# A log-softmax that streams 3.3 GB through one DMA queue: one store in four sent as two halves around the next load

## The chip, the core and the metric

The kernel runs on one core of one Trainium2 chip. The core has a matrix engine (PE), a vector engine (DVE), a scalar engine (ACT), a general-purpose engine (POOL) and a sync engine (SP), which here issues all transfers. Transfers are carried by 16 DMA engines. The metric is device time in microseconds; the time of a kernel is the median of its runs.

## The reference

For an array `x` of 16 × 512 rows of 50000 float32 numbers:

```python
def reference(x):
    max_x = np.max(x, axis=-1, keepdims=True)
    shifted = x - max_x
    log_sum_exp = np.log(np.sum(np.exp(shifted), axis=-1, keepdims=True))
    return (shifted - log_sum_exp).astype(np.float32)
```

The input is 1638.4 MB and so is the output. Every number is read once and written once.

## The kernel before

**Tiles.** The 8192 rows are cut into 256 tiles of 32 rows. A row is spread over four of the 128 partitions, so a tile is 128 partitions × 12500 numbers (50,000 bytes in a partition, 6250 KB in all). Four buffers (`bufs[0]` to `bufs[3]`) hold four tiles; tile t lives in buffer t mod 4, and the result overwrites the input in place.

**Compute.** For each tile DVE waits until it has landed, takes the negated maximum of four pieces of 3125 columns (`negm`, L206), combines them over the four partitions of each row (L211, L174 to L189), and later subtracts maximum and log-sum in one instruction over the whole tile (L194). ACT takes the exponentials with their sums (L242), the scale factors (L250) and the logarithm (L236). PE adds the sums over the partitions of a row (L270). DVE goes from one tile to the next strictly in order.

**Transfers.** SP runs a program written out by hand (L151 to L167). It loads the first four tiles and stores tile 0. Then a loop of 63 rounds follows with four steps each. Step j, with k the next buffer after j, does this, in this order: wait until buffer k's result is ready (`subtracted[k]`), issue its store; wait until the store of buffer j, issued one step earlier, has completed (`stored[j]`, which counts 16 for one transfer); issue the load of a new tile into buffer j. All waits go through one helper, `take` (L45), which waits for a count and subtracts it. SP does one thing after the other: while it waits, nothing behind the wait is issued. Transfers of SP go into one queue. I write S1 for the store of buffer 1 and L0 for the load of buffer 0; a round is then S1 L0 S2 L1 S3 L2 S0 L3. After the loop the last tiles are stored, the very last one in four pieces of 3125 columns.

Of the kernel before, what the change touches and what calls it, by code (L numbers as in the profile page):

```python
# [42 lines left out]
def take(engine, sem, n=16):  # L43

    engine.wait_ge(sem, n).then_inc(sem, -n)  # L45


def cols(c):
    return slice(c * C, (c + 1) * C)
# [3 lines left out]
def kernel(  # L53
# [9 lines left out]
    W = V // G  # L63
# [10 lines left out]
    def run(a, first, n):  # L74

        part = a[first : first + NBUF * n].rearrange("(q i) p w -> q i p w", i=NBUF)
        return lambda q, i: part[bass.ds(q, 1), i].rearrange("o p w -> (o p) w")
# [13 lines left out]
    bufs = [data.tile([P, W], FP32, name=f"buf{j}") for j in range(NBUF)]  # L91
# [19 lines left out]
    def sem(name):  # L111
        return ctx.enter_context(nc.semaphore(name))

    landed = [sem(f"landed{j}") for j in range(NBUF)]
    stored = [sem(f"stored{j}") for j in range(NBUF)]
# [13 lines left out]
    @block.gpsimd  # L129
    def _(gpsimd):  # L130
        view = ones.rearrange("p (r g) -> p r g", g=G)
        gpsimd.memset(ones, 1.0).then_inc(ready)  # L132
        gpsimd.affine_select(  # L133
            out=view, in_=view, pattern=[[-G, R], [0, G]], base=0,
            channel_multiplier=1, compare_op=ALU.is_ge, fill=0.0,
        ).wait_op(ready, 1, "sem-ge").then_inc(ready)
        gpsimd.affine_select(  # L137
            out=view, in_=view, pattern=[[G, R], [0, G]], base=G - 1,
            channel_multiplier=-1, compare_op=ALU.is_ge, fill=0.0,
        ).wait_op(ready, 2, "sem-ge").then_inc(ready)  # L140

    @block.sync
    def _(sync):
        def load(j, src):
            sync.dma_start(out=bufs[j], in_=src).then_inc(landed[j], 16)

        def store(j, dst, buf):
            take(sync, subtracted[j], 1)
            sync.dma_start(out=dst, in_=buf).then_inc(stored[j], 16)

        for t in range(NBUF):  # L151
            load(t, xt[t])
        store(0, ot[0], bufs[0])
        src, dst = run(xt, NBUF, rounds), run(ot, 1, rounds)
        with sync.Fori(0, rounds) as q:
            for j in range(NBUF):
                k = (j + 1) % NBUF
                store(k, dst(q, j), bufs[k])
                take(sync, stored[j])
                load(j, src(q, j))  # L160
        for j in range(1, NBUF - 1):
            store(j, ot[ntiles - NBUF + j], bufs[j])
        for c in range(NS):
            store(NBUF - 1, ot[ntiles - 1][:, cols(c)], bufs[NBUF - 1][:, cols(c)])
        for j in range(NBUF - 1):
            take(sync, stored[j])
        take(sync, stored[NBUF - 1], 16 * NS)  # L167
# [147 lines left out]
```

## Time and profile before

| what | value |
|---|---|
| median of 5 runs | 7593.84 us (7593.16 to 7594.87) |
| profiled execution | 7593.36 us |
| its span, first to last instruction | 7591.7 us |
| DVE busy | 5440.2 us, 72% |
| ACT busy | 3184.7 us, 42% |
| PE busy | 477.9 us, 6% |
| HBM read and written | 1638.40 MB each, 432 GB/s over the span |
| SP's waits in `take` (L45) | 7301.9 us in 512 waits |

The page gives busy time by engine, then the span in 40 slices with the busy share of the DMA engines in tenths and the rate, then the DMA queues (packets, MB, share of the time of 16 engines), groups of instructions by line, and the transfers by kind with their size and the median time from issue to landing. The timeline lists instructions in order of time: start, duration, engine, line, operation, and in brackets the idle time before it and who ended it. A packet is one contiguous piece moved by one DMA engine: 50,000 bytes, one partition's share of a tile. A transfer of 128 partitions gives each of the 16 engines eight of them, followed by one small packet that adds 1 to the transfer's semaphore.

### The profile page before, as it was taken

What the parts mean: (1) busy time and instruction counts of PE and PEld (TensorE: products, weight loads), DVE (VectorE), ACT (ScalarE), POOL (GpSimd) and SP (SyncE); (2) the same over time, 40 slices, a digit from 0 to 9 for tenths busy, and PEclk for the clock granted to TensorE, in tenths of its full rate; (3) what the DMA queues carried; (4) which work ended last, traced back from release to release, by engine and by line L of the source; (5) the groups of instructions that cost most, each with busy time, mean ns of one, the idle gap of its engine ahead of it and who ended that gap; (6) DMA issues with size and microseconds to landing.
All of it is one profiled execution on the core that took longest, in us unless ns stands there. A gap on an engine that the chain in (4) does not pass through costs nothing. (4 is left out here: it accounts for less than half of the span.)

```text
span 7591.7 us, 14139 instructions
## 1 busy us (share of the span) xinstructions
PE 477.9 (6%) x2048; PEld 455.9 (6%) x2048; DVE 5440.2 (72%) x2819; ACT 3184.7 (42%) x2561; POOL 1.4 (0%) x7
## 2 busy tenths in 40 slices
PE   0000000000000000000000000000000000000000
PEld 0000000000000000000000000000000000000000
DVE  7777777777777777777777777777777777777776
ACT  4444443434444344443444434444344443434433
POOL 0000000000000000000000000000000000000000
DMA  9999999999999999999999999999999999999999
GB/s 425 432 432 433 432 434 433 432 433 433 432 433 433 433 433 433 433 432 434 432 434 432 434 433 433 433 433 433 433 432 433 433 433 433 433 433 433 433 433 392
DMA packets 74162, 3276.85 MB, mean 432 GB/s; under 512 B 8240, under 2 KB 8240, under 8 KB 8240
## 3 DMA queue, kind: packets, MB, share of 16 engines
q1 hardware_dynamic: 74160, 3276.83, 100.0%
q14 instruction: 2, 0.02, 0.0%
HBM read 1638.40 MB, written 1638.40 MB: 432 GB/s over the span
## 5 line engine op out<-in xcount | busy, mean ns | idle before, releaser
L242 ACT ACTIVATE dump<-buf,negm 128x3125 f32<-128x3125 f32 x1024 | 2937.2, 2868 | 3804.2 <-DVE negm L206 3706.7
L206 DVE TENSOR_REDUCE negm<-buf 128x1 f32<-128x3125 f32 x1024 | 3418.3, 3400 | 922.7 <-DVEq L45 922.7
L194 DVE TENSOR_SCALAR buf<-buf,negmax,logsum 128x12500 f32<-128x12500 f32 (+1 forms) x259 | 1738.8, 6715 | 554.0 <-ACT logsum L236 554.0
L270 PE MATMUL sums<-scaled,ones 128*128 128x1 f32 x2048 | 477.9, 355 | 7086.6 <-DVE scaled L217 7086.6
L270 PEld LDWEIGHTS sums<-scaled,ones 128*128 128x128 f32 x2048 | 455.9, 328 | 7108.4 <-DVE scaled L217 7108.4
L217 DVE TENSOR_TENSOR scaled<-scale,part 128x4 f32<-128x4 f32 x256 | 41.4, 162 | 580.4 <-ACT scale L250 580.4
L236 ACT ACTIVATE logsum<-sums 128x1 f32<-128x1 f32 x256 | 43.8, 171 | 551.1 <-PE sums L270 551.1
L242 ACT ACTIVATION_READ_ACCUMULATOR dump<-buf,negm 128x1 f32 x1024 | 190.9, 186 | 0.0
L250 ACT ACTIVATE scale<-negm,negmax 128x4 f32<-128x4 f32 x256 | 76.1, 297 | 23.6
L211 DVE TENSOR_REDUCE negp<-negm 128x1 f32<-128x4 f32 x256 | 40.1, 157 | 39.2 <-DVE negm L206 39.2
L189 DVE STREAM_TRANSPOSE negmax<-spread 128x32 f32<-128x32 f32 x256 | 54.2, 212 | 8.9
L174 DVE STREAM_TRANSPOSE allneg<-negp 128x32 f32<-128x32 f32 x256 | 54.1, 211 | 8.9
L177 DVE TENSOR_REDUCE rowneg<-allneg 128x8 f32<-128x32 f32 x256 | 47.5, 186 | 8.9
L183 DVE COPY spread<-rowneg 128x32 f32<-128x32 f32 x256 | 46.3, 181 | 8.9
L257 ACT ACT_TABLE_LOAD x1 | 1.3, 1283 | 1.0 <-SPq L109 1.0
L137 POOL TENSOR_SCALAR_AFFINE_SELECT ones<-ones 128x128 f32<-128x128 f32 x1 | 0.5, 518 | 0.1
L133 POOL TENSOR_SCALAR_AFFINE_SELECT ones<-ones 128x128 f32<-128x128 f32 x1 | 0.5, 517 | 0.1
L132 POOL MEMSET ones<- 128x128 f32 x1 | 0.2, 204 | 0.5 <-SPq L109 0.5
L299 POOL MEMSET const-bfloat16-1.0<- 128x1 bf16 x1 | 0.1, 101 | 0.0
L299 POOL MEMSET const-uint8-127<- 128x1 uint8 x1 | 0.1, 101 | 0.0
L299 POOL MEMSET const-float32-0.0<- 128x1 f32 x1 | 0.1, 98 | 0.3 <-issue 0.3
L299 POOL MEMSET const-float32-1.0<- 128x1 f32 x1 | 0.1, 98 | 0.0
## 6 DMA issues: line engine op xcount, KB each, us to landing
buf<-in_x_dram SPq DMA_DIRECT2D x256, 6250.0 KB, 44.2
out_dram<-buf SPq DMA_DIRECT2D x255, 6250.0 KB, 47.8
out_dram<-buf SPq DMA_DIRECT2D x4, 1562.5 KB, 11.7
```

What stands on the lines that cost most here:

```text
L174: vector.transpose(out=allneg, in_=negp.to_broadcast([P, SQ]))
L177: vector.tensor_reduce(out=rowneg, in_=allneg.rearrange("p (r g) -> p r g", g=G), op=ALU.min, axis=AX,)
L183: vector.tensor_copy(out=spread.rearrange("p (r g) -> p r g", g=G), in_=rowneg[:, :, None].to_broadcast([P, SQ // G, G]),)
L189: vector.transpose(out=negmaxs[k], in_=spread)
L194: ins = vector.tensor_scalar(out=buf, in0=buf, scalar1=negmaxs[k][:, 0:1], scalar2=logs[k], op0=ALU.add, op1=ALU.subtract,)
L206: vector.tensor_reduce(out=negms[j][:, c : c + 1], in_=bufs[j][:, cols(c)], op=ALU.max, axis=AX, negate=True,).then_inc(shifted.sem if c < ...
L211: vector.tensor_reduce(out=negp, in_=negms[j], op=ALU.min, axis=AX).then_inc(on_dve.sem)
L217: vector.tensor_mul(out=scaleds[j], in0=scales[j], in1=parts[j])
L236: scalar.activation(out=logs[k], in_=rowsums[k], func=ACT.Ln)
L242: scalar.activation(out=dump, in_=bufs[j][:, cols(c)], func=ACT.Exp, bias=negms[j][:, c : c + 1], scale=1.0, accum_out=parts[j][:, c : c + 1],
L250: scalar.activation(out=scales[j], in_=negms[j], func=ACT.Exp, bias=negmaxs[j][:, 0:1], scale=-1.0,)
L270: ins = tensor.matmul(rowsums[j], ones, scaleds[j][:, c : c + 1], start=c == 0, stop=c == NS - 1,)
```

## The change

In step j=0 of each round, the store of buffer 1 is issued as two transfers, columns 0 to 6249 and columns 6250 to 12499. The first is issued where the whole store was. The second is issued after the load of buffer 0. Both add to `stored[1]`, so the wait of step j=1, ahead of the load into buffer 1, is for 32 instead of 16. The order in a round becomes S1a L0 S1b S2 L1 S3 L2 S0 L3. Nothing else differs: not the compute engines' programs, and not what SP does before and after the loop.

```diff
         src, dst = run(xt, NBUF, rounds), run(ot, 1, rounds)
+        half = [slice(0, W // 2), slice(W // 2, W)]
         with sync.Fori(0, rounds) as q:
             for j in range(NBUF):
                 k = (j + 1) % NBUF
-                store(k, dst(q, j), bufs[k])
-                take(sync, stored[j])
+                if j == 0:
+                    store(k, dst(q, j)[:, half[0]], bufs[k][:, half[0]])
+                else:
+                    store(k, dst(q, j), bufs[k])
+                take(sync, stored[j], 32 if j == 1 else 16)
                 load(j, src(q, j))
+                if j == 0:
+                    sync.dma_start(
+                        out=dst(q, j)[:, half[1]], in_=bufs[k][:, half[1]]
+                    ).then_inc(stored[k], 16)
```

## The prediction

> **What bounds the kernel now.** I read the page from its second part, because no engine of the first part is near full (DVE 72%).
>
> ```profile
> span 7591.7 us, 14139 instructions
> ...
> DMA  9999999999999999999999999999999999999999
> GB/s 425 432 432 433 432 434 433 432 433 433 432 433 433 433 433 433 433 432 434 432 434 432 434 433 433 433 433 433 433 432 433 433 433 433 433 433 433 433 433 392
> ...
> q1 hardware_dynamic: 74160, 3276.83, 100.0%
> ...
> buf<-in_x_dram SPq DMA_DIRECT2D x256, 6250.0 KB, 44.2
> out_dram<-buf SPq DMA_DIRECT2D x255, 6250.0 KB, 47.8
> out_dram<-buf SPq DMA_DIRECT2D x4, 1562.5 KB, 11.7
> ```
>
> The 16 DMA engines are busy in every slice, at one rate, and all of it is the one queue q1. A transfer is 6250 KB and lands 44 to 48 us after its issue, while 432 GB/s moves it in 14.8 us: three transfers stand in line. The order of issue, one round of the loop (the SP part of the timeline of 3008 to 3128 us; columns are start, duration, instruction):
>
> ```profile
> 3008.49 0.34 SPq L149 DMA_DIRECT2D out_dram<-buf  x1
> 3026.84 0.35 SPq L145 DMA_DIRECT2D buf<-in_x_dram  x1
> 3038.09 0.34 SPq L149 DMA_DIRECT2D out_dram<-buf  x1
> 3056.49 0.35 SPq L145 DMA_DIRECT2D buf<-in_x_dram  x1
> 3067.73 0.34 SPq L149 DMA_DIRECT2D out_dram<-buf  x1
> 3086.11 0.35 SPq L145 DMA_DIRECT2D buf<-in_x_dram  x1
> 3097.29 0.34 SPq L149 DMA_DIRECT2D out_dram<-buf  x1
> 3115.76 0.35 SPq L145 DMA_DIRECT2D buf<-in_x_dram  x1
> 3127.03 0.34 SPq L149 DMA_DIRECT2D out_dram<-buf  x1
> ```
>
> 101 stores were issued before the first row, so it is store number 101, counted from 0: buffer 1, step j=0. The rows are S1 L0 S2 L1 S3 L2 S0 L3, then S1 again 118.54 us later. That is eight transfers of 14.82 us; the DMA sets the period. The vector engine has slack in it, which its own rows show for one tile:
>
> ```profile
> 3001.45 6.79 DVE L194 TENSOR_SCALAR buf<-buf,negmax,logsum 128x12500 f32<-128x12500 f32 x1 [2.17 <-ACT logsum L236]
> ...
> 3011.89 13.35 DVE L206 TENSOR_REDUCE negm<-buf 128x1 f32<-128x3125 f32 x4 [3.65 <-DVEq L45]
> ```
>
> After each subtraction DVE waits 3.65 us for the next tile to land (the wait on `landed`, taken at L45).
>
> **One DMA engine is behind the other fifteen.** A transfer ends with sixteen small semaphore packets, one for each engine. In the trace's landing events fifteen engines lead the last one by 2 to 4 us in the first rounds, by 11 us at most in round 40, by 18 us in round 62: 0.30 us a round. Its packets follow each other every 1850.7 ns on average, those of the others every 1846.5 (single packet records around 7150 us). So the end belongs to this engine, and the tail shows it alone. The DMA view of 7583 to 7589 us:
>
> ```profile
> DMA packets 14, 0.16 MB, mean 27 GB/s; under 512 B 1, under 2 KB 1, under 8 KB 1
> ## 3 DMA queue, kind: packets, MB, share of 16 engines
> q1 hardware_dynamic: 14, 0.16, 6.4%
> ```
>
> 6.4% of 16 engines is one engine. Its whole run adds up to the span: first packet at 2.0 us, 511 whole transfers of 14.82 us (7573), four quarter stores 15.14, then 1.9 us to the span's end: 7592 against 7591.7. Whatever lengthens this engine's packets is paid in full; whatever only moves instructions is paid nothing as long as its ring has work.
>
> **The change, part by part.**
>
> 1. *63 more DMAs, in 63 rounds.* Store 1 becomes two, of 25,000 B a row in place of 50,000. Each DMA engine gets 16 half rows instead of 8 whole ones, and one semaphore packet more. No half row is in the trace; the nearest row is the last tile, stored in four quarters of 12,500 B. On the lagging engine its four semaphore packets follow that of the store before it by 3.788, 3.783, 3.800 and 3.773 us: 15.144 us for a tile. Whole stores on the same engine take 14.86 us in steady state (semaphore packet at 7200.30 to 7215.15). The difference, 0.28 us, pays for 24 more row pieces and 3 more semaphore packets; a half split adds 8 and 1, a third: 0.095 us. On the other engines a quarter row takes 471.2 ns to the next packet, a whole one 1846.5: (4 × 471.2 − 1846.5)/3 = 12.8 ns a piece, × 8, + 6 ns for the semaphore packet (9 ns long, 3 overlapped) = 0.108 us. I take 0.10 us a round: 63 × 0.10 = **6.3 us**. Lower bound: the shortest quarters (464 ns) against the shortest wholes (1843 ns) give 4.3 ns a piece, 0.041 us a round, 2.6 us. Upper bound: quarter rows were stored with no loads beside them for the most part, half rows will be stored beside loads on other engines; I allow double, 0.2 us, 12.6 us. The quarters begin at offsets 12,500, 25,000 and 37,500 B in a row, so the halves' offset is among them, and is no dearer there.
>
> A rule that speaks against the change: the Trainium skill, "DMA: Bandwidth & Descriptors", Anatomy of one DMA, gives about 2.0 us fixed for every DMA, most of it the wait until the last write is confirmed. Paid here, that is 63 × 2.0 = 126 us, and 7720 us. The trace disagrees: on the busy ring the packet after a semaphore packet starts 6 ns after that packet's start, and packets overlap by 3 ns. With transfers in line the receipt of one lies under the next. I take the row, and keep the rule for a ring that runs empty.
>
> 2. *Load 0 goes ahead of half a store.* In the queue: before S1 L0 S2 L1, after S1a L0 S1b S2 L1. The bytes before S2 are the same, so S2 and all behind it keep their places. L0 lands 7.4 us earlier (36.8 us after issue instead of 44.2). DVE can use 3.65 us of that, since it is busy until then; S0's subtraction ends about 3093.6 instead of 3097.2, S0 is still behind L2 (issued 3086.1) in line, and then DVE waits some 7.3 us for tile 1, which lands no earlier. Gain: nothing. Changes of direction between load and store stay eight a round. SP's one more issue (0.34 us) falls in its waits: SP waited 7301.9 us of the span.
>
> 3. *The wait for 32 moves the issue of load 1.* S1b lands where L0 landed, about 3071.0, so L1 is issued at 3071.2 instead of 3056.49, 14.7 us later. Queued behind that wait on SP: L1, then S3, whose subtraction is done at 3067.7; S3 goes out at about 3071.6, 3.9 us late. L2's own wait, for S2 at 3085.7, is not moved. What covers this is S2, issued at 3038.09 and served from 3071.0 to 3085.8: the lagging engine has 14.6 us of work when L1 is issued, and L1 needs about 1.0 us from issue to first packet (first load: issued 1.04, first packet 2.04; first quarter store on idle engines: 7566.66 to 7567.50, 0.84). L1 then takes its old place. S3 has S2's rest and L1 before it, 29 us. Cost nothing; without the cover, up to 1.0 us a round, 63 us. The fifteen leading engines have less: with a lead over 14.6 us, from about round 50, they run dry for 0.3 us a round. They are ahead of the one that sets the end, so this costs nothing.
>
> 4. *First rounds and tail.* In round 0, S1a is issued at 71 us, L0 at 79.3, S1b lands at about 106, S2 (96.97) is in line: L1 at 107 instead of 97.56, again under S2. No transfer behind the loop is touched.
>
> **Sum:** +6.3 us on the span, 7591.7 to 7598.0; the profiled execution was 7593.36 and the median of the runs 7593.84, 0.48 above it, so 7593.84 + 6.3 = **7600.1 us**, +0.08%. About 0.2% (15.2 us) is what a measurement of this kernel can tell from no change.
>
> **Rivals.** *The pieces cost nothing:* the second half's row starts are hidden under the engine's own reads; 7594 to 7596. For it: the shortest quarters; against: their mean. *Slower, the late load:* L1 is issued with one transfer ahead instead of two. If that transfer did not suffice, because descriptors must lie in the ring earlier than I think, the lagging engine would be dry each round; it decides from 0.24 us a round (15.2/63), and at a whole first-packet time of 1.0 us gives 7593.8 + 6.3 + 63 = 7663. Against it: 14.6 us of cover against 1.0. *Slower, dearer half rows:* between loads a half row costs more than a quarter row by itself. From 0.24 us a round it decides: 15 ns more for each of 16 half rows; a doubling of that, 0.48 us, gives 7624. Against it: quarters stored while the lagging engine was still on whole rows show 463 to 500 ns each. *Faster:* with the others held back the lagging engine speeds up; if it lost its whole excess of 4.2 ns a packet it would gain 17 us, 7583 with the pieces paid. Against it: it was as slow in the first rounds, when no lead had grown.
>
> **How the numbers follow.** Pieces at 0.04 to 0.2 us a round: 0.80. Nothing: 0.06, also within 0.2%. Late load 0.05, dearer half rows 0.06, faster 0.03. So faster 0.03, same 0.86, slower 0.11. The time is the likeliest's, 7600.1. The range takes in the lower bound and part of "nothing" (7595.5), and goes up to where "slower" begins (7609), a little past double price, 7606.4; that leaves some 0.18 out.
>
> **What would show it.** Packets of q1: 74160 + 63 × 144 = 83232, 9248 of them under 512 B; stores as x192 of 6250 KB and x126 of 3125 KB. A round of SP's rows of 118.6 us, L0's issue at once followed by S1b's, L1's about 14.7 us later in the round. DVE's wait before L206 gone for one tile in four and about 7.3 us for the next. GB/s still 432. Wrong if the DMA row falls to 8, if half rows take much over 930 ns, or if L1's landing moves in the round.

## The result and the profile after

The changed kernel takes 7604.33 us (median of 27 runs, 7602.12 to 7607.35) against 7594.08 us for the kernel before (47 runs, 7592.82 to 7596.40). The ratio is 1.0013, with a 95% interval of 1.0008 to 1.0018: 10.25 us slower. The forecast was 7600.1 us, between 7595.5 and 7609.0, and "same within 0.2%" as the likeliest class. Both held. But the added time was forecast at 6.3 us, so two fifths of it came from somewhere else.

The page after the change:

```profile
span 7603.1 us, 14328 instructions
...
DMA  9999999999999999999999999999999999999999
GB/s 424 433 431 433 432 433 432 432 433 433 432 433 432 434 432 432 433 433 434 433 432 432 433 433 432 431 431 430 429 432 430 431 433 432 431 431 430 431 432 401
...
q1 hardware_dynamic: 83232, 3276.84, 100.0%
...
buf<-in_x_dram SPq DMA_DIRECT2D x256, 6250.0 KB, 40.6
out_dram<-buf SPq DMA_DIRECT2D x192, 6250.0 KB, 47.9
out_dram<-buf SPq DMA_DIRECT2D x126, 3125.0 KB, 40.9
out_dram<-buf SPq DMA_DIRECT2D x4, 1562.5 KB, 11.7
```

The packet count is exactly the one worked out beforehand (83232), and the DMA row is full everywhere. The rate shows something that the forecast had not: from slice 26 on it is more often 430 or 431 than 433. The kernel before had 433 there. The rate is that of all 16 engines; what the last of them loses is counted below.

One round of the order of issue, from the SP part of the timeline of 3000 to 3128 us (start, duration, instruction):

```profile
3012.03 0.33 SPq L149 DMA_DIRECT2D out_dram<-buf  x1
3030.38 0.35 SPq L145 DMA_DIRECT2D buf<-in_x_dram  x1
3030.92 0.33 SPq L166 DMA_DIRECT2D out_dram<-buf  x1
3041.62 0.33 SPq L149 DMA_DIRECT2D out_dram<-buf  x1
3074.85 0.35 SPq L145 DMA_DIRECT2D buf<-in_x_dram  x1
3075.45 0.37 SPq L149 DMA_DIRECT2D out_dram<-buf  x1
3089.78 0.35 SPq L145 DMA_DIRECT2D buf<-in_x_dram  x1
3097.07 0.33 SPq L149 DMA_DIRECT2D out_dram<-buf  x1
3119.41 0.35 SPq L145 DMA_DIRECT2D buf<-in_x_dram  x1
```

These rows are S1a, L0, S1b, S2, L1, S3, L2, S0, L3. L1 goes out 44.47 us after L0. In the kernel before it was 29.65, so L1 is 14.8 us late (forecast 14.7); S3 follows it at once, and L2 is in its old place. The vector engine's waits show where the tiles land (brackets: idle time before the row, and who ended it):

```profile
3015.41 13.35 DVE L214 TENSOR_REDUCE negm<-buf 128x1 f32<-128x3125 f32 x4 [3.63 <-DVEq L45]
3045.06 13.35 DVE L214 TENSOR_REDUCE negm<-buf 128x1 f32<-128x3125 f32 x4 [3.67 <-DVEq L45]
3070.95 13.35 DVE L214 TENSOR_REDUCE negm<-buf 128x1 f32<-128x3125 f32 x4
3104.47 13.35 DVE L214 TENSOR_REDUCE negm<-buf 128x1 f32<-128x3125 f32 x4 [7.56 <-DVEq L45]
```

The wait at the earlier-landing tile 0 has gone (the third row has no bracket), and the next tile's wait is 7.56 us. Forecast: gone, and 7.3. So far the trace follows the prediction.

**The lagging engine, transfer by transfer.** Sixteen landing events end a transfer, and the last of them belongs to the lagging engine. The time from one such last event to the next is what that engine spends on the transfer. Medians in us over 18 or 19 rounds each (1900 to 4100 us), worked out from the landing events in the traces, with the kernel "adj" of the first experiment, which sends both halves one behind the other:

| | before | adj | after |
|---|---|---|---|
| store 1, whole or both halves | 14.890 | 15.002 in all | 7.486 + 7.494 |
| load 0 | 14.740 | 14.740 | 14.743 |
| store 2 | 14.875 | 14.876 | 14.922 |
| L1, S3, L2, S0, L3 together | 74.029 | 74.026 | 74.029 |
| round | 118.534 | 118.644 | 118.674 |

A store's landing event comes about 0.03 us later than a load's: a load's packets take 14.77 us on this engine, while its interval, measured from a store's event, is 14.74. So store 2 of the kernel before, measured from a load's event, truly takes 14.845; in the changed kernel, measured from a store's event, it takes 14.922. It lost 0.08 us. And the two halves of store 1 carry the 0.03 twice, so the split itself costs 0.06 us of the 0.09 that the table shows. The packet records, which need no such correction, give the same: from one semaphore packet of this engine to its next, store 2 takes 14.847 us in the kernel before and 14.927 in the changed one, and store 1 takes 14.866 against 7.463 + 7.463. Nothing else in the round moved. The added 0.140 us times 63 rounds is 8.8 of the 10.25 us.

These rounds are early ones. By the last landing of load 3, the changed kernel's profiled execution falls behind that of the kernel before by 0.17 us a round in rounds 7 to 42, and by 0.26 in rounds 42 to 63. So there is a further term, and most of it is late.

### The profile page after: what moved, and what is told of

Read it like the earlier page. It is cut to its first block, busy times and chain, and to the rows that moved or that the text cites. A ratio compares the mean times of both kernels' runs of the same rounds, so it can differ in the third digit from the quotient of the medians.

```text
span 7603.1 us, 14328 instructions
## 1 busy us (share of the span) xinstructions
PE 477.9 (6%) x2048; PEld 456.0 (6%) x2048; DVE 5434.7 (71%) x2819; ACT 3184.6 (42%) x2561; POOL 1.4 (0%) x7
## 3 DMA queue, kind: packets, MB, share of 16 engines
q1 hardware_dynamic: 83232, 3276.84, 100.0%
## 6 DMA issues: line engine op xcount, KB each, us to landing
out_dram<-buf SPq DMA_DIRECT2D x4, 1562.5 KB, 11.7
```

## The experiments

Three theories stood at the start. A: the whole +10 us is the price of 63 more transfers. B: the pieces cost what was forecast or less, and the rest is store 2, which stands directly behind a store instead of behind a load. C: the rest comes from the fifteen leading engines, which run into the end of their ring once their lead is as large as L1's late issue allows. All kernels below still compute the whole output.

**adj: the halves one behind the other, the load after both**

```diff
                 if j == 0:
+                    take(sync, subtracted[k], 1)
+                    part(k, dst(q, j), 0)     # columns 0:6250
+                    part(k, dst(q, j), 1)     # columns 6250:12500
                 else:
                     store(k, dst(q, j), bufs[k])
+                take(sync, stored[j], 32 if j == 1 else 16)
                 load(j, src(q, j))
```

> Both halves of store 1 go out one behind the other, then the load as before: S1a S1b L0 S2 L1. L1 is issued when the whole of store 1 has landed, with L0 and S2 ahead of it, as in the kernel before. Theory A (the prediction's sum, only with a dearer piece): the whole +10 us is the price of 63 more transfers; this gives +10 us. Theory B (the pieces cost what was predicted, 6 us, and the rest is store S2, which stands directly behind store S1b on the lagging DMA engine's ring and takes 14.93 us there instead of 14.85): +6 us if only a store behind a whole store counts, up to +11 if half S1b behind half S1a counts as well. Theory C (the pieces cost 6 us, the rest is the leading engines running dry because L1 comes late): +6 us, and the lead of the other engines grows to 18 us as in the kernel before.

Measured: 7600.64 us against 7594.28, +6.4 us, ratio 1.0008 (1.0000 to 1.0016). The lead grew to 16.1 us by round 56, as in the kernel before. Theory A falls: the same 63 extra transfers cost 4 us less here. (The intervals of the two ratios overlap; the times hardly do, 7599.51 to 7602.34 against 7602.12 to 7607.35.) The 0.10 us forecast for a pair of halves is what a pair costs when the second half stands behind the first: the table's 15.002 − 14.890 = 0.11. By the packet records the half behind a load takes 7.471 us and the half behind a half store 7.507.

**late: no split, load 0 ahead of store 1**

```diff
                 if j == 0:
+                    take(sync, stored[j])
+                    load(j, src(q, j))
+                    store(k, dst(q, j), bufs[k])
```

> No store is split. In step 0 load 0 goes ahead of the whole store 1: L0 S1 S2 L1. L1 is issued as late as in the changed kernel, with only S2 ahead, and S2 stands directly behind S1. Theory A: 0 us. Theory B: 63 x 0.08 = +5 us, from the first rounds on, with S2 at 14.93 us on the lagging engine. Theory C: +2 to +4 us, and only after round 40 or so, when the lead reaches the 12 to 15 us that L1's late issue allows; before that a round takes 118.53 us as in the kernel before.

Measured: 7614.39 us, +20.1 us, ratio 1.0026 (1.0016 to 1.0037). All three theories were too low. The first rounds explain 6 us of it, by a fault of this experiment: in round 0 nothing may be issued until store 0 has landed. The page's first slice is at 412 GB/s against 425, and SP's rows are

```profile
45.27 0.34 SPq L149 DMA_DIRECT2D out_dram<-buf  x1
80.26 0.35 SPq L145 DMA_DIRECT2D buf<-in_x_dram  x1
80.86 16.64 SPq L149 DMA_DIRECT2D out_dram<-buf  x2
```

with store 1, ready at 71 us, going out at 80.86 behind an empty ring. The remaining 14 us are spread over all rounds, 0.25 us each. S2 behind S1 has a median of 14.922 us, which is theory B's mark, with no split anywhere. But S1, now behind two loads in a row, also takes 14.944 instead of 14.890, which no theory had, and in the later rounds the mean of L0 rises from 14.79 to 14.84. So B's effect is there and not alone.

**alt: store 1 and load 0 both in halves, sent in turn**

```diff
+                    part(k, dst(q, j), 0)
                     take(sync, stored[j])
+                    load_half(j, src(q, j), 0)
+                    part(k, dst(q, j), 1)
+                    load_half(j, src(q, j), 1)
```

> Store 1 and load 0 are both cut in halves and sent in turn: S1a L0a S1b L0b S2 L1. There are 126 more transfers (and one for the first load), no store directly behind a store, and L1 has 22 us of transfers ahead of it. Theory A: twice 10, +20 us. Theory B and theory C: only the pieces, twice 6, +12 to +13 us, spread over all rounds alike; the lead grows to 18 us as in the kernel before.

Measured: 7626.96 us (7619.76 to 7642.81), +32.7 us, ratio 1.0042 (1.0028 to 1.0056). No theory had this. The profiled run was the slowest, 7642.81, so the losses below are larger than those of the median run. Rate by fortieths of its span:

```profile
GB/s 424 432 430 433 432 432 433 431 432 433 431 433 432 433 432 431 434 432 433 433 431 434 432 432 433 432 433 432 431 431 428 426 427 427 426 426 424 416 422 374
```

In rounds 14 to 41 it loses 0.21 to 0.34 us a round against the kernel before, for two splits. From about round 45, when the lead is 19.6 to 20 us, it loses 1.6 us a round, and in the last seven rounds 3.1. L1 has 22 us of transfers ahead of it here, and the lead stops growing, so the leading engines may have reached the end of their ring. That would be theory C's mark, much larger than C had it; theory B has nothing for it. It is not shown: in "adj4" below the last engine loses time at the same lead although nothing stops the others.

**dry: the changed kernel with store 2 issued after load 1**

```diff
+                elif j == 1:
+                    take(sync, stored[j], 32)
+                    load(j, src(q, j))
+                    store(k, dst(q, j), bufs[k])
```

> The changed kernel with store 2 issued after load 1 instead of before it, so that nothing is in line when L1 is issued: S1a L0 S1b, then the wait for both halves, then L1 S2. It measures what L1's late issue costs once its cover is gone. By the row of the first load (1.0 us from issue to first packet) plus the time from the last packet to SP's wake-up of 0.2 us: 63 x 1.2 + 10 = +86 us. By the fixed 2.0 us per DMA that the skill's page states: 63 x 2.0 + 10 = +136 us. The lead of the fifteen engines is then lost in every round.

Measured: 7963.15 us, +368.9 us, ratio 1.0484 (1.0470 to 1.0499), 5.9 us a round. SP's rows around L1, and the DMA view of 3090 to 3100 us, of which a column is a quarter of a microsecond:

```profile
3049.47 0.33 SPq L157 DMA_DIRECT2D out_dram<-buf  x1
3094.88 0.35 SPq L145 DMA_DIRECT2D buf<-in_x_dram  x1
3095.49 0.92 SPq L149 DMA_DIRECT2D out_dram<-buf  x2
```

```profile
DMA  9966992242000200000000099950000009994400
GB/s 800 400 300 300 700 400 100 100 200 100 0 0 0 100 0 0 0 0 0 0 0 0 0 1600 1000 400 200 0 0 0 0 0 0 400 1400 1000 200 200 0 0
```

(Packets are counted where they begin.) After the last pieces of S1b no engine begins a packet until L1's first ones, all together, just before 3096 us. In the packet records all sixteen are idle for 1.57 us in each round. That is near the forecast 1.2, but the interval from S1b's landing to L1's is 19.3 us instead of 14.8, 4.5 more: another 2.9 us go into the engines' unequal start (0.9 us from the first to the last in the round shown) and into L1's own packets. Of an engine's eight packets of L1, the first takes 2.65 us and the last 2.94 (means of 17 rounds); the six between take the usual 1.847. Over the run 9% of the 50,000-byte packets take more than 1900 ns, with 1% above 3000. The lead stays at 1 to 3 us. Both forecasts for "dry" missed these long packets. That they come from the engines' starting together was not tested.

**first_half and second_half: the change in only one half of the rounds**

```diff
+        mid = 32
+        with sync.Fori(0, mid) as q:            # changed rounds in first_half
...
+        with sync.Fori(0, rounds - mid) as q:   # changed rounds in second_half
```

> The change in rounds 0 to 31 only; rounds 32 to 62 are those of the kernel before. Pieces: 32 x 0.10 = 3.2 us. Theory B (S2 directly behind half S1b costs the lagging engine 0.05 to 0.08 us in every changed round): 1.6 to 2.6 us more, 5 to 6 us in all. Theory C (L1 comes too late for the leading engines once their lead has reached the 12 us it allows): nothing more, because the lead is 10 us when the change ends, and it then grows on to about 18 us: 3 to 4 us in all.

> Rounds 0 to 31 are those of the kernel before, the change is made in rounds 32 to 62. Pieces: 31 x 0.10 = 3.1 us. Theory B: 5 to 6 us in all, the same as with the first half. Theory C: the lead is 9 us when the change begins and is stopped at about 12 us some 8 rounds later; from there a round takes 118.8 us or more instead of 118.62, so 3.1 + 23 x 0.17 = 7 us in all, and packets over 1900 ns appear only there.

Measured against 7594.62: first half 7599.16, +4.5 us, ratio 1.0006 (0.9997 to 1.0014); second half 7599.88, +5.3 us, ratio 1.0007 (0.9999 to 1.0015). Together they make 9.8 of the change's 10.25 us, so the price is spread over both halves. (The first half's 4.5 lies between B's forecast, 5 to 6, and C's, 3 to 4; the second's is B's.) In both, S2 behind S1b has the median 14.922. In the second half the lead stops at 11.9 us, and there alone the means lie above the medians: sum of means 118.71 us, of medians 118.64. The two intervals overlap, so the 0.8 us between the halves proves nothing by itself. Theory C's 7 us did not come in the median, though the interval does not shut it out.

**pairs: S1 S2 L0 L1**

```diff
+                if j < 2:
+                    store(k, dst(q, j), bufs[k])
+                    if j == 0:
+                        continue
+                    for i in range(2):
+                        take(sync, stored[i])
+                        load(i, src(q, i))
```

> No store is split and no load waits longer for its cover: in steps 0 and 1 together S1 S2 L0 L1 is issued instead of S1 L0 S2 L1. L1 has S2 and L0 ahead of it, 29 us, as in the kernel before; L0 comes 15 us later in line, which the vector engine's slack of 3.65 us a tile takes up over the round. Theory B: S2 stands behind S1, and L1 behind L0: 63 x 0.08 = +5 us, in all rounds alike. Theory C: 0 us, and the lead grows to 18 us.

Measured: 7629.31 us, +34.7 us, ratio 1.0045 (1.0031 to 1.0058). Theory B had forecast +5. It is no test of B, because its cover is not what its text says: L0 now waits in SP's program behind store 2's subtraction. S2, the second of the two merged stores, goes out at 3060.5 and L0 at 3061.04 (start, duration):

```profile
3034.57 26.22 SPq L149 DMA_DIRECT2D out_dram<-buf  x2
3061.04 11.51 SPq L145 DMA_DIRECT2D buf<-in_x_dram  x2
```

Only what was left of S1 stood in line when S2 and L0 went out. The lead stopped at 9.1 us by round 30, and from there 3.3% of the packets took over 1900 ns and a round cost 0.5 us more. What stays of use is S2 behind S1, 14.963 us, again more than behind a load, and the sign that a shorter line costs more.

**gate: the old order, with L1 held back until a small load behind L0 has landed**

```diff
                 take(sync, stored[j], 32 if j == 1 else 16)
                 load(j, src(q, j))
+                if j == 0:
+                    sync.dma_start(out=tick, in_=xt[0][0:16, 0:128]).then_inc(stored[1], 16)
```

> The order of the kernel before, S1 L0 S2 L1, but a small load of 16 rows of 512 bytes into an unused tile stands behind L0, and L1 waits for it as well as for S1. L1 is issued when L0 has landed, with S2 alone ahead, as late as in the changed kernel; no store is split, and no store stands behind a store. The small load adds one packet of 512 bytes and a semaphore packet to each engine in a round, about 0.05 us, 3 us in all. Theory B: +3 us, nothing else. Theory C: +3 us until the lead reaches about 12 us (round 40), then 0.1 to 0.2 us a round more: +5 to +7 us, and the lead stops there.

Measured: 7599.99 us against 7594.62, +5.4 us, ratio 1.0007 (0.9998 to 1.0015). The small load costs the lagging engine 0.05 us (L0 to S2 by way of it 0.193 + 14.731, instead of 14.875), 3.1 us in all, and in rounds 21 to 34 the whole round is up by just that. From round 42 on, with the lead at 11.7 to 11.9 us, it is up by 0.10. So L1's late issue, with no split and no store behind a store, costs about 0.05 us a round once the lead is used up, some 1 us over the run, and nothing before. The rest of the 5.4 us lies in rounds 7 to 20, where no theory expects it: the total is in theory C's range, but for the most part not for C's reason.

**double: the change for stores 1 and 3**

```diff
-                if j == 0:
+                if j % 2 == 0:                  # split, second half after the load
-                take(sync, stored[j], 32 if j == 1 else 16)
+                take(sync, stored[j], 32 if j % 2 else 16)
```

> The change made twice a round, for stores 1 and 3: S1a L0 S1b S2 L1 S3a L2 S3b S0 L3. From the landing intervals of the lagging engine so far, one change costs it 0.056 us for the pieces and 0.08 us for the store that stands directly behind a store, in all rounds: 126 x 0.136 = 17 us. The lagging engine then falls back by 0.57 us a round, so the lead reaches the 12 us that the late loads allow at about round 20, and the remaining 43 rounds cost 0.05 to 0.1 us more for each late load: 4 to 9 us. Together +21 to +26 us. If the pieces cost 0.10 us and nothing else is to be paid: +12.6 us.

Measured: 7611.94 us against 7594.75, +17.2 us, ratio 1.0022 (1.0014 to 1.0031). The forecast 21 to 26 us did not come. That is 17 us for the pieces and the stores behind stores, and nothing on top. The lead reached 11.9 us by round 32 and stopped there. S2 and S0, each behind a half store, have medians of 14.922 and 14.944; S1a, S1b, S3a and S3b are 7.46 to 7.49. Theory A's price of 10 us a change would have given 20, the pieces alone 12.6.

**adj4: every store of the loop in two adjacent halves**

```diff
+                part(k, dst(q, j), 0)
+                part(k, dst(q, j), 1)
+                take(sync, stored[j], 32)
                 load(j, src(q, j))
```

> All stores of the loop cut in halves, sent one behind the other, with every load as early as in the kernel before: S1a S1b L0 S2a S2b L1 and so on. 253 more transfers. By the one pair a round (+6.4 us, 0.10 us a pair): 253 x 0.10 = +25 us, in all rounds alike, with the lead growing to 18 us or more and hardly a packet over 1900 ns in the later rounds.

Measured: 7622.45 us, +27.7 us, ratio 1.0036 (1.0022 to 1.0049), 0.109 us for each of 253 pairs. Packets over 1900 ns were 0.4% after 5400 us. The price of an adjacent pair is the same for one or four in a round: in rounds 7 to 56 of the profiled execution it is 0.110 us. But the price was not alike in all rounds, as had been expected. In the last seven, with the lead growing from 20 to 27 us, the lagging engine's round rises from 118.93 to between 119.3 and 119.9 us, while that of the others stays at 118.61. The profiled run was the slowest of the five (7626.41). Why the last engine slows down there was not found.

**Packets over 1900 ns.** They are the trace left where the leading engines run into the end of their ring. Share of the 50,000-byte packets, from the packet records, with the lead at round 56:

```
kernel    1500-4500 us   5400-7400 us   lead, us
before        0.34%          0.06%        16.1
adj           0.53%          0.08%        16.1
gate          0.49%          2.49%        11.8
after         0.44%          3.11%        12.0
double        1.27%          3.16%        11.8
alt           0.74%          4.88%        20.0
dry           9.35%          8.53%         1.8
```

Wherever L1's late issue has stopped the lead, two to five in a hundred packets are long, and where it is free to grow almost none. In the changed kernel this begins at about round 35, which is slice 23 of the page, and the lower rates follow a few slices later: most of that is the fifteen engines falling to the pace of the last.

The place of these packets points to L1. Between 5400 and 7300 us, 334 of the changed kernel's 441 start within 20 us after a landing of S1b, the moment at which L1 is issued. The engines hardly stand idle there, about 0.2 us a round summed over all sixteen; what they give up is in the long packets, 8.5 us a round over all sixteen. The lagging engine meets few of them, but some: 12 of 870 of its packets that could be followed between 5400 and 7400 us (six of the 12 in S2), against none of 1032 in the kernel before. Their excess over 1848 ns makes 2.0 us in 17 rounds, 0.12 us a round, which is about the size of the late term.

## Why the prediction held, and where its sum failed

*What bounds the kernel* was right: the end belongs to one DMA engine, and all that counted was what that engine spends on its packets. That the result lies inside the range is in part luck: the room above 6.3 us was left for dearer half rows, which did not come, and other terms used it.

*Part 1, the pieces, 0.10 us a round.* As a price of an adjacent pair it is confirmed to the tenth of a microsecond (adj +6.4 us, forecast 6.3; adj4 0.109 us a pair). But that price has two terms in it. It was taken from four quarter stores that stand behind each other, and so it holds a store behind a store as well. With a load between the halves, as in the change, the split costs 0.06.

*Part 2, "S2 and all behind it keep their places" and "gain: nothing", is the step that failed.* It counted bytes and changes of direction, found both unchanged, and did not ask what each transfer stands behind. S2 used to follow a load and now follows S1b, a store. It takes 14.922 instead of 14.845 us on the lagging engine, in the changed kernel, in both half versions, in late and in double. In adj, where S2 still follows a load, and in gate, where L1 is late but S2 follows loads, it does not. 63 × 0.08 = 5 us. Why a store is dearer behind a store stays open. The row was in the trace of before: in the tail, where S1 and S2 stand behind each other, the lagging engine takes 14.97 us for S2 against 14.86 for a store of the loop. The prediction used the semaphore packets just after that store and passed over it.

*Part 3, L1's late issue.* Its times were right (14.8 us late, under S2, S3 right behind it), and so was the place where the leading engines are stopped; the lead stopped at 12 us, from about round 37, forecast 14.6 us and round 50. They lose time in long packets and not, as forecast, by standing dry. That this costs nothing is not quite right: "gate" shows about 0.05 us a round, the lagging engine's long packets 0.12, over some 25 rounds, and what is left of the change's 10.25 us after 8.8 is 1.4 us. "double" shows no such cost. I leave this term between 0 and 3 us. Why "alt" loses 1.6 to 3 us a round at its end, where the lead is 20 us, was not found.

*The price without cover* was far off: at most 1.0 us a round by the first-packet time, 2.0 us by the skill's fixed price of a DMA, and 5.9 measured. Both leave out the long packets behind the stop. The cover of 14.6 us held, so this did not touch the result; the rival "late load", whose worst case was put at 7663, would have ended at 7963.

*The skill's 2.0 us for each DMA, weighed in part 1 against the row:* the Trainium skill, "DMA: Bandwidth & Descriptors", Anatomy of one DMA, gives this figure for transfers issued from the general-purpose engine, not for "every DMA", as the prediction has it; all transfers here come from SP. adj bears the row out: 63 more transfers cost 0.10 us each on a ring with work, and 253 more 0.11 each in adj4.

The sum with the measured terms: 63 × (0.06 + 0.08) = 8.8, and 1.4 us, which the late long packets can account for: 10.25. The 6.3 of the forecast came near it because the split was put too high (0.10 for 0.06) and the store behind a store at nothing.

## What to carry to other kernels

When a kernel is bound by DMA, find out whether all DMA engines end together; if one lags, price a change in that engine's packets, and only there. When a transfer is moved, look up what each neighbour will stand behind, not only whether the bytes and the order are kept: the same store cost 0.5% more behind a store than behind a load. And keep work in line: in the changed kernel and in "gate" a wait that left the ring one transfer deep cost about 0.1 us a round at most; in "dry" one that emptied it cost 5.9.

## What the runs showed of the hardware that was not expected

- On the lagging engine a store takes 14.85 us and a load 14.77; the fifteen others, followed over nine rounds (3000 to 4100 us), take 14.77 and 14.78 us for the two kinds. So it lags in its stores alone. Why this one differs was not tried.
- A 6250 KB store directly behind a store takes 14.92 us there in the changed kernel, its two halves, late and double, and 14.96 in pairs; behind a load it takes 14.845. Behind two loads in a row it takes 14.92 as well (late: 14.925 by the packet records; one kernel only).
- After a common stop on an empty ring, the first and the last of the eight packets of the next load took 2.65 and 2.94 us in place of 1.85 on all engines ("dry"). Together with the unequal start this cost more (2.9 us) than the time in which all sixteen were idle (1.57 us).
